# A hybrid attention block: rows of q and k renumbered for their set-down, rotary tables made early

## The chip, the cores and the metric

The kernel runs on one core of a Trainium2 chip. A core has five engines that each work through their own list of instructions in order: TensorE (PE) for matrix products, VectorE (DVE), ScalarE (ACT), GpSimd (POOL) and SyncE (SP), which here issues every transfer (DMA). The engines wait for one another by semaphores. The metric is the device time of one execution in microseconds (us).

## The reference, cut to what matters

The block has two sub-layers over 1024 tokens of width 1024. The first normalises x, scales and shifts it by a vector computed from the conditioning input c (a product with `w_ada`), projects it, and runs two kinds of attention side by side: mixer A (8 query heads, 2 key heads, a sliding window of 128, a sink in the softmax) and mixer B (8 heads, a mixture of three dilated windows). In each head the first 16 of 64 entries of q and k are rotated by the token's position:

```python
def partial_rope(x, cos, sin):
    half = ROT_DIM // 2
    x1 = x[..., :half].astype(jnp.float32)
    x2 = x[..., half:ROT_DIM].astype(jnp.float32)
    rot = jnp.concatenate([x1 * cos - x2 * sin, x2 * cos + x1 * sin], axis=-1).astype(x.dtype)
    return jnp.concatenate([rot, x[..., ROT_DIM:]], axis=-1)
```

The mixers' outputs are normalised, joined and projected, and the result is added to x. The second sub-layer is a squared-ReLU perceptron of width 4096, also scaled, shifted and gated from c. Scores are sums over a head's 64 entries, so the order in which these entries lie in memory is free as long as q and k agree.

## The kernel before, in words

All products are done in split precision: an operand is held as a rounded part (hi) and its rest (lo), and a product is three matmuls, hi x hi, lo x hi and hi x lo (lines 861, 862 and 864 in the projection).

*Front.* The first 36 us or so load x and part of `w_ada`, normalise x (ACT's squares at line 613, POOL's power for the root), transpose it on PE (`pxt`), and form the scale and shift in four groups (`acc_a`, `pm`, `g_a`, `s_a`). ACT and DVE then write the modulated input `hw` (lines 681, 684, 687). While PE has no work, it multiplies ones (`ones_r`).

*Units.* Attention is done in six units: 0 and 1 are mixer A (4 query heads and one key head each), 2 to 5 mixer B (2 heads each). A unit's projection has three column groups c = 0, 1, 2 for each half x of the sequence (512 tokens). The first unit accumulates in six banks at once (`acc`), the others one bank after another (`pj`). Columns are ordered by `_columns()` such that c = 0 holds all entries that are rotated. Weights are loaded (`w_st`), rounded on ACT (line 539) and their rests formed on DVE or POOL (line 544).

*Evacuation and set-down.* `evac` takes each bank to a staging tile (`stage`, five buffers): for c = 0 DVE rotates (lines 757 to 760, with the tables `tabs`), ACT rounds (763), DVE or POOL forms the rest (766); for c = 1 and 2 ACT rounds (774) and DVE forms the rest (777). Then SP moves rows out of the staging tile into `qt` and `kt`, with entries along the partitions and the hi and lo parts in two blocks of 64 partitions (line 803). This is called a set-down below. The staging buffer is free again when its set-down has landed. The lists `PARTS_A` and `PARTS_B` say which staging rows go where: first row, count, step, q or k, first row of the head.

```python
o = dst[64 * i + row:64 * i + row + m_].bitcast(F32)
nc.sync.dma_start(o, src if both else src[:, s_])
```

*Rotary tables.* DVE reduces the angles at the start. `f_sin` takes sine and cosine on ACT and then one exponential, since ACT holds one set of functions at a time and softmax needs the other. POOL writes sine and cosine into row tiles (`rows`, line 713), PE transposes them (`ptab`, line 719) and ACT scales them into `tabs` (721). They are made once for the A units and again for the B units.

*Attention* takes scores (`s_ps`: line 1177 for A, 1122 for B), softmax over DVE, ACT and POOL, transposes (`pt_ps`) and the product with v (`o_ps`); results go to memory by way of `ot` and `o_dram`. POOL also reduces the remaining `w_ada` pieces (`wa_st`, `ada_acc`), whose loads share the staging buffers. After about 560 us the perceptron follows (`mlp_ps`), in which PE is the only limit.

*Order.* No order is written out by hand. The class `Sched` simulates the engines with assumed durations when the program is built, and emits each engine's work in the order of that simulation, so a change in one place shifts the order elsewhere. It counts a transfer by its bytes at one rate, whatever rows it goes to (lines in `load`).

Of the kernel before, what the change touches and what calls it, by code (L numbers as in the profile page):

```python
# [19 lines left out]
P = 128  # L20
# [13 lines left out]
def _split_const(value, top, bits, count):  # L34
    parts, rest, unit = [], value, 2.0 ** (top - bits)
    for _ in range(count):
# [29 lines left out]
PARTS_B = (((0, 64, 2, "q", 0), (1, 64, 2, "k", 0)), ((0, 64, 2, "q", 32), (1, 64, 2, "k", 32)), ())  # L66
PARTS_A = (((0, 32, 2, "q", 0), (64, 32, 2, "q", 32), (1, 64, 2, "k", 0)),
           ((0, 96, 1, "q", 8), (96, 32, 1, "q", 40)), ((0, 64, 1, "q", 48),))

ROWS_B = [*range(0, 8), *range(16, 24), *range(8, 16), *range(24, 64)]  # L70
ROWS_A = [*range(0, 8), *range(16, 40), *range(8, 16), *range(40, 64)]


def _columns():

    out = []
    for u in range(6):
        if u > 1:
            q = [512 + 128 * u + 64 * h for h in range(2)]
            k, v = [x + 512 for x in q], [x + 1024 for x in q]  # L80
            parts, rows = PARTS_B, ROWS_B
        else:
            g = u
            q, k, v = [256 * g + 64 * h for h in range(4)], [512 + 64 * g], [640 + 64 * g]
            parts, rows = PARTS_A, ROWS_A
        for c in range(3):
            got = [h + d for h in v for d in range(64)] if c == 2 else []
            got = [0] * (P - len(got)) + got
            for p, n, step, whose, row in parts[c]:
                heads = q if whose == "q" else k  # L90
                got[p:p + n * step:step] = [h + rows[row + r] for r in range(n // len(heads)) for h in heads]
            out += got
    return out
# [226 lines left out]
def t_sb(n):  # L320
    return 0.098 + 0.00083 * n
# [27 lines left out]
def hybrid_block(ctx: ExitStack, tc: tile.TileContext, x, positions, w_ada, b_ada, g_attn_post, w_in, w_out,  # L349
# [227 lines left out]
    e_cond = op("DVE", 0.52, f_cond, [e], prio=0)  # L577

# [25 lines left out]
    def f_sin():  # L604
        A.activation(sinw[:, :, 1], ang[:], AF.Sin)
        A.activation(cosw[:], kq[:], AF.Sin)
        A.activation(ang[:], kq[:], AF.Exp)
    e_ang, e_xn = e, [[], []]

    def x_block(tb):  # L610
# [4 lines left out]
        e = rsqrt_mean(rstd[:, tb:tb + 1], ssq[:, tb:tb + 1], e)  # L615
        e = op(("ACT", "DVE"), (t_sb(D) + AP_COST, t_d2(D) + AP_DV),
# [77 lines left out]
    for g in range(4):  # L694
        mod_group(g)
    e = op("ACT", 3.2, f_sin, [e_ang] + e_xn[0] + e_xn[1], prio=8)
    e_rope = op("DVE", 0.15, lambda: V.tensor_scalar(sinw[:, :, 0], sinw[:, :, 1], -1.0, None, ALU.mult), [e],
                prio=8)

    def tables(groups, place, r_place, r_bank, bank, deps):  # L700

        for i in range(2):
            b = {}

            def f_rows(i=i, b=b):
                t = b["t"] = place()[:].rearrange("p (b r) -> p b r", b=TB)
                G.memset(t, 0.0 if i else 1.0)
                for o, step, h in groups:
                    for x in range(2):
                        src = sinw[:, :, 1 - x] if i else cosw[:]  # L710
                        o_ = o + 64 * x
                        for j in range(h):
                            G.tensor_copy(t[:, :, o_ + j * step:o_ + j * step + (8 * h - h) * step + 1:h * step], src)
            e = op("POOL", 4.0, f_rows, [e_rope], takes=[(r_place, 1)], prio=0)
            for x in range(2):
# [4 lines left out]
                d = pe_op("tab", 0.43, f_t, [e], takes=[(r_bank, 1)], gives=[(r_place, 1)] if x else [])  # L720
# [5 lines left out]
    tables([(0, 2, 4), (1, 2, 1)], lambda: place0("rows"), r_wa, r_t,  # L726
           lambda: pt.tile([P, 4, P], F32, name="ptab", tag="t"), [[], []])


# [4 lines left out]
    def evac(u, x, c, get_ps, done, r_bank):  # L734
# [47 lines left out]
        if parts:  # L782
            for whose in ("k", "q") if c == 0 else ("q", "k"):
# [5 lines left out]
                for s_ in ((0, 1) if not both else (None,)):  # L789
                    new = c == 0 and whose == "k" and s_ in (0, None)  # L790

                    def f_st(s_=s_, new=new, mine=mine, whose=whose, nh=nh, both=both):
# [5 lines left out]
                        for p0_, n_, step, _, row in mine:  # L798
                            src = b["f"][p0_:p0_ + (n_ - 1) * step + 1:step]
                            m_ = n_ // nh  # L800
                            for i in range(2) if both else (s_,):
                                o = dst[64 * i + row:64 * i + row + m_].bitcast(F32)
# [138 lines left out]
    def feed_proj():  # L941
        if len(sc.pe.get("dense", [])) <= 4 and todo_dense:
# [3 lines left out]
            if (u, x, c) == (2, 0, 0):  # L946
                for e_ in e_tab:
                    e_.clear()
                tables([(0, 1, 4)], lambda: stage("rows"), r_stg, r_x,
# [1125 lines left out]
```

## Time and profile before

| quantity | value |
|---|---|
| median of three runs | 1163.08 us (1161.61 to 1167.61) |
| the profiled execution | 1161.99 us |
| its span in the trace | 1160.2 us |
| PE busy | 1117.1 us, 96% of the span |
| DVE busy | 815.4 us, 70% |
| ACT busy | 639.2 us, 55% |
| POOL busy | 261.1 us, 23% |

The page lists each engine's busy time, the granted clock of PE over the span, the chain of work that ended last, and groups of instructions. Lines such as L803 are lines of the kernel before; in the changed kernel lines behind the first edits are up to five higher. A row in a list of instructions gives start, duration, engine, line, operation and tiles, and in brackets the idle time before it with what ended it. Matmuls overlap, so the duration of one (390 ns) is longer than the distance between two (some 230 ns).

### The profile page before, as it was taken

To read this page: it belongs to the slowest core of one execution; us is meant where nothing else is said; L and a number is where in the kernel's file an instruction comes from. 1 tells how busy PE (TensorE), PEld (TensorE's weight loads), DVE (VectorE), ACT (ScalarE), POOL (GpSimd) and SP (SyncE) were. 2 spreads that over 40 slices of the span, in tenths; PEclk is the share of its full clock that TensorE was granted. 3 is DMA by queue.
4 is the path that set the end of the run, shared out by engine and by line. 5 is a ranking of instruction groups with operands and counts; after the bars stand their busy time and mean duration, and the time that the engine had idled before them with its cause. 6 is when DMAs were issued, how large, how long until landed. Compare 5 with 4: busy or idle time off the path is not lost.

```text
span 1160.2 us, 15646 instructions
## 1 busy us (share of the span) xinstructions
PE 1117.1 (96%) x5416; PEld 926.6 (80%) x5416; DVE 815.4 (70%) x1380; ACT 639.2 (55%) x1105; POOL 261.1 (23%) x344
## 2 busy tenths in 40 slices
PE   8989989999999899998999999999999999999996
PEld 7768778788888787887788888888888888888885
DVE  7848576566666775658969665499653796547998
ACT  7949676455555774667676524563233732246542
POOL 2347667566663441112000000000000000000002
PEclk9989989999999989999999999999999999999998
DMA  9477857465545614554683057812369212585103
GB/s 351 161 174 168 168 120 182 111 153 122 134 102 130 156 48 139 193 181 182 257 314 118 19 207 274 315 50 89 120 220 326 106 55 73 184 306 181 37 19 146
DMA packets 90944, 185.31 MB, mean 160 GB/s; under 512 B 8432, under 2 KB 31088, under 8 KB 90864
## 3 DMA queue, kind: packets, MB, share of 16 engines
q1 hardware_dynamic: 90864, 184.30, 51.1%
q8 instruction: 43, 0.70, 0.3%
q14 instruction: 37, 0.30, 0.1%
HBM read 137.08 MB, written 28.31 MB: 143 GB/s over the span
## 4 chain that ended last, share of the span: by engine, by line
PE 70%; DVE 10%; DMA 7%; issue 4%; POOL 4%; ACT 3%; SPq 2%; DVEq 0%; POOLq 0%; ACTq 0%
PE mlp_ps L1898 16%; PE mlp_ps L1899 16%; PE mlp_ps L1897 16%; PE pj L861 3%; PE pj L864 3%; PE pj L862 3%; PE s_ps L1122 2%; PE o_ps L1257 1%; DMA wa<-in_w_ada 1%; SPq L803 1%; PE pt_ps L1227 1%; DMA wa_st<-in_w_ada 1%; DVE hw L1668 1%; PE pt_ps L1230 1%; PE s_ps L1177 1%
## 5 line engine op out<-in xcount | busy, mean ns | idle before, releaser
L1897 PE MATMUL mlp_ps<-hw 128*128 128x512 f32 x896 | 349.7, 390 | 1.2 <-ACT hw L1659 1.2
L1898 PE MATMUL mlp_ps<-hw 128*128 128x512 f32 x896 | 348.7, 389 | 1.1 <-DVE hw L1665 1.1
L1899 PE MATMUL mlp_ps<-hw 128*128 128x512 f32 x896 | 348.6, 389 | 0.0
L1897 PEld LDWEIGHTS mlp_ps<-hw 128*128 128x128 f32 x896 | 168.2, 188 | 36.8 <-ACT hw L1659 1.6
L1898 PEld LDWEIGHTS mlp_ps<-hw 128*128 128x128 f32 x896 | 168.2, 188 | 36.8 <-DVE hw L1665 1.4
L1899 PEld LDWEIGHTS mlp_ps<-hw 128*128 128x128 f32 x896 | 168.2, 188 | 34.9
L1668 DVE TENSOR_TENSOR hw<-w,hw 128x1024 fp32r<-128x1024 f32 x96 | 114.5, 1219 | 94.7 <-ACT hw L1661 94.4
L1661 ACT CAST hw<-w 128x1024 fp32r<-128x1024 f32 x96 | 97.5, 1047 | 129.8 <-PE mlp_ps L1899 97.5
L1997 POOL TENSOR_TENSOR st<-st,nhalf 128x1 f32<-128x1 f32 x8 | 7.8, 978 | 601.9 <-DVE st L1995 601.9
L861 PE MATMUL pj<-hw,w_hl 128*128 128x512 f32 x240 | 104.2, 434 | 0.0
L864 PE MATMUL pj<-hw,w_hl 128*128 128x512 f32 x240 | 95.5, 398 | 0.0
L862 PE MATMUL pj<-hw,w_hl 128*128 128x512 f32 x240 | 95.3, 397 | 0.0
L1245 DVE TENSOR_TENSOR ph<-pt_ps,ph 128x512 fp32r<-128x512 f32 (+1 forms) x110 | 69.7, 648 | 36.0 <-ACT ph L1241 35.7
L1661 ACT CAST hw<-u 128x1024 fp32r<-128x1024 f32 x48 | 48.7, 1052 | 64.6 <-PE mlp_ps L1899 64.6
L1241 ACT CAST ph<-pt_ps 128x512 fp32r<-128x512 f32 (+1 forms) x110 | 59.5, 555 | 32.1 <-PE pt_ps L1230 27.0
L1668 DVE TENSOR_TENSOR hw<-u,hw 128x1024 fp32r<-128x1024 f32 x48 | 57.0, 1218 | 18.2 <-ACT hw L1661 18.2
L1148 ACT ACTIVATE p_sb<-p_sb,mn 128x128 f32<-128x128 f32 (+3 forms) x64 | 49.7, 777 | 36.3 <-DVE mn L1141 34.9
L1955 DVE TENSOR_TENSOR yacc<-yacc,mlp_ps 128x512 f32<-128x512 f32 x96 | 62.1, 681 | 3.3 <-PE mlp_ps L1899 3.3
L1153 POOL TENSOR_SCALAR p_sb<-p_sb,den 128x128 f32<-128x128 f32 (+3 forms) x64 | 49.0, 775 | 47.8 <-DVE den L1151 44.6
L1010 POOL TENSOR_TENSOR ada_acc<-ada_acc,wa_st 128x512 f32<-128x512 f32 x42 | 55.5, 1320 | 3.5
L864 PEld LDWEIGHTS pj<-hw,w_hl 128*128 128x128 f32 x240 | 45.6, 190 | 10.7
L1473 PE MATMUL y_ps<-hw,oh 128*128 128x512 f32 x128 | 51.7, 404 | 0.0
(205 smaller groups left out, 2010.6 us busy)
## 6 DMA issues: line engine op xcount, KB each, us to landing
hw<-s_dram SPq DMA_DIRECT2D x84, 512.0 KB
wa_st<-in_w_ada SPq DMA_DIRECT2D x32, 512.0 KB
w<-in_w_up SPq DMA_DIRECT2D x32, 512.0 KB
w<-in_w_down SPq DMA_DIRECT2D x32, 512.0 KB
s_dram<-hw SPq DMA_DIRECT2D x28, 512.0 KB
w_st<-in_w_in SPq DMA_DIRECT2D x36, 256.0 KB
x_sb<-in_x SPq DMA_DIRECT2D x16, 512.0 KB
wa<-in_w_ada SPq DMA_DIRECT2D x32, 256.0 KB
```

Of the source, the lines that this page charges most:

```text
L861: T.matmul(ps, w[:, 0, n], h[0], start=(k == 0), stop=False)
L862: T.matmul(ps, w[:, 1, n], h[0], start=False, stop=False)
L864: T.matmul(ps, w[:, 0, n], h[1], start=False, stop=(k == KC - 1))
L1010: G.tensor_tensor(ada.acc[:, :512], ada.acc[:, :512], wa[:, j], ALU.add)
L1241: A.copy(b["ph"][:, 0, :w], b["pt"][:, :w])
L1245: V.tensor_tensor(b["ph"][:, 1, :w], b["pt"][:, :w], b["ph"][:, 0, :w].bitcast(F32), ALU.subtract)
L1661: A.copy(out[j][0], flat(src[j]))
L1668: V.tensor_tensor(out[j][1], flat(src[j]), out[j][0].bitcast(F32), ALU.subtract)
L1897: T.matmul(ps[m][:], sh, mh, start=starts and k == 0, stop=False, **kw)
L1898: T.matmul(ps[m][:], sh, ml_, start=False, stop=False, **kw)
L1899: T.matmul(ps[m][:], sl, mh, start=False, stop=k == 3, **kw)
L1955: e = op("DVE", t_dv(512), lambda: V.tensor_tensor(y(), y(), ps[m][:], ALU.add), [e, ml.e_y[tb, n]], gives=gives, prio=1)
```

## The change

It has two parts.

The rows of q and k are renumbered. hi and lo no longer lie in two blocks of 64 partitions but in turn, row by row, and the rows that one transfer fills are 2, 4 or 8 partitions apart and reach over all 128. A sixth entry in `PARTS_A` and `PARTS_B` gives the distance, `ROWS_A` and `ROWS_B` reorder the weights' columns to match, and the key head of mixer A's rotary rows in the tables moves likewise. For mixer A the two or three pieces of q in a column group become one, so there are fewer transfers; for mixer B their number stays.

The rotary tables are made early. ACT loads the sine functions at the start, ahead of the first square of x, by a small activation on `warm`; `f_sin` follows as soon as the angles are reduced and is without the exponential, which a second small activation fetches behind the last modulation. The tables' row tiles lie in the ring of the values (`vring`) instead of the front's buffers, are written once all roots of x are known, and PE transposes them after the fourth modulated block.

```diff
-PARTS_B = (((0, 64, 2, "q", 0), (1, 64, 2, "k", 0)), ((0, 64, 2, "q", 32), (1, 64, 2, "k", 32)), ())
-PARTS_A = (((0, 32, 2, "q", 0), (64, 32, 2, "q", 32), (1, 64, 2, "k", 0)),
-           ((0, 96, 1, "q", 8), (96, 32, 1, "q", 40)), ((0, 64, 1, "q", 48),))
...
-ROWS_B = [*range(0, 8), *range(16, 24), *range(8, 16), *range(24, 64)]
-ROWS_A = [*range(0, 8), *range(16, 40), *range(8, 16), *range(40, 64)]
+PARTS_B = (((0, 64, 2, "q", 0, 2), (1, 64, 2, "k", 0, 2)), ((0, 64, 2, "q", 1, 2), (1, 64, 2, "k", 1, 2)), ())
+PARTS_A = (((0, 64, 2, "q", 0, 4), (1, 64, 2, "k", 0, 1)), ((0, 128, 1, "q", 1, 2),), ((0, 64, 1, "q", 2, 4),))
+
+FIRST_B = [*range(0, 8), *range(16, 24), *range(8, 16), *range(24, 32)]
+ROWS_B = [FIRST_B[r // 2] if r % 2 == 0 else 32 + r // 2 for r in range(64)]
+ROWS_A = [r // 4 if r % 4 == 0 else 16 + 3 * (r // 4) + r % 4 - 1 for r in range(64)]
...
-            for p, n, step, whose, row in parts[c]:
+            for p, n, step, whose, row, ds in parts[c]:
                 heads = q if whose == "q" else k
-                got[p:p + n * step:step] = [h + rows[row + r] for r in range(n // len(heads)) for h in heads]
+                got[p:p + n * step:step] = [h + rows[row + ds * r] for r in range(n // len(heads)) for h in heads]
...
+    warm = p0.tile([P, KC], F32, name="warm")
+    e_sinset = op("ACT", 1.5, lambda: A.activation(warm[:], nhalf[:], AF.Sin), [e, e_init], prio=0)
...
@@ -604,8 +606,10 @@
     def f_sin():
         A.activation(sinw[:, :, 1], ang[:], AF.Sin)
         A.activation(cosw[:], kq[:], AF.Sin)
-        A.activation(ang[:], kq[:], AF.Exp)
-    e_ang, e_xn = e, [[], []]
+    e_xn, e_rs = [[], []], []
+    e_sin = op("ACT", 0.5, f_sin, [e, e_sinset], prio=1)
+    e_rope = op("DVE", 0.15, lambda: V.tensor_scalar(sinw[:, :, 0], sinw[:, :, 1], -1.0, None, ALU.mult), [e_sin],
+                prio=1)
...
         e = op("ACT", t_sb(D) + AP_COST, f_sq, [x_e[tb]], prio=2)
         e = rsqrt_mean(rstd[:, tb:tb + 1], ssq[:, tb:tb + 1], e)
+        e_rs.append(e)
...
-    e = op("ACT", 3.2, f_sin, [e_ang] + e_xn[0] + e_xn[1], prio=8)
-    e_rope = op("DVE", 0.15, lambda: V.tensor_scalar(sinw[:, :, 0], sinw[:, :, 1], -1.0, None, ALU.mult), [e],
-                prio=8)
...
             def f_rows(i=i, b=b):
-                t = b["t"] = place()[:].rearrange("p (b r) -> p b r", b=TB)
+                t = b["t"] = place(i)
                 G.memset(t, 0.0 if i else 1.0)
...
-            e = op("POOL", 4.0, f_rows, [e_rope], takes=[(r_place, 1)], prio=0)
+            e = op("POOL", 4.0, f_rows, [e_rope] + e_rs, takes=[(r_place, 1)] if r_place else [], prio=0)
             for x in range(2):
                 def f_t(x=x, b=b):
                     b[x] = bank()
                     for j in range(4):
                         T.transpose(b[x][:, j], b["t"][:, 4 * x + j], ident)
-                d = pe_op("tab", 0.43, f_t, [e], takes=[(r_bank, 1)], gives=[(r_place, 1)] if x else [])
+                d = pe_op("tab", 0.43, f_t, [e, e_hh[3, 1]], takes=[(r_bank, 1)], gives=[(r_place, 1)] if x and r_place else [])
...
-    tables([(0, 2, 4), (1, 2, 1)], lambda: place0("rows"), r_wa, r_t,
+    tables([(0, 2, 4), (1, 8, 1)], lambda i: vring.tile([P, TB, P], F32, name="rows", tag="v"), r_v, r_t,
            lambda: pt.tile([P, 4, P], F32, name="ptab", tag="t"), [[], []])
...
+    op("ACT", 1.6, lambda: A.activation(warm[:], nhalf[:], AF.Exp), [e_sin] + [e_hl[KC - 1, x] for x in range(2)],
+       prio=8)
...
                         dst = qs[u, x][:] if whose == "q" else ks[u][:, :, cs]
-                        for p0_, n_, step, _, row in mine:
+                        for p0_, n_, step, _, row, ds in mine:
                             src = b["f"][p0_:p0_ + (n_ - 1) * step + 1:step]
                             m_ = n_ // nh
                             for i in range(2) if both else (s_,):
-                                o = dst[64 * i + row:64 * i + row + m_].bitcast(F32)
+                                o = dst[2 * row + i:2 * row + i + 2 * ds * (m_ - 1) + 1:2 * ds].bitcast(F32)
                                 nc.sync.dma_start(o, src if both else src[:, s_])
...
-                tables([(0, 1, 4)], lambda: stage("rows"), r_stg, r_x,
+                tables([(0, 1, 4)], lambda i: stage("rows")[:].rearrange("p (b r) -> p b r", b=TB), r_stg, r_x,
                        lambda: px.tile([P, 4, P], F32, name="ptab", tag="x"), [[e_rot[1, 0]], [e_rot[1, 1]]])
```

How the order of instructions moves shows at three places. The first is SP's queue, the set-down of the first unit (kt and qt are k and q as scores read them, hl the staging tile; sizes are partitions x elements). Before, for the first half, from the masks on:

```order
L971 DMA masks<-in_consts 128x1280
L530 DMA w_st<-in_w_in 128x512
L994 DMA wa_st<-in_w_ada 128x2x512
L803 DMA kt<-hl 64x2x512 x2
L803 DMA qt<-hl 8x4x512 x4
L803 DMA qt<-hl 24x4x512
L803 DMA qt<-hl 8x4x512
L803 DMA qt<-hl 24x4x512
L803 DMA qt<-hl 8x4x512
L803 DMA qt<-hl 16x4x512 x2
```

Now, for the same half:

```order
L976 DMA masks<-in_consts 128x1280
L530 DMA w_st<-in_w_in 128x512 x3
L808 DMA kt<-hl 64x2x512 x2
L808 DMA qt<-hl 16x4x512 x2
L808 DMA qt<-hl 32x4x512 x2
L808 DMA qt<-hl 16x4x512 x2
```

Twelve issues become eight, the load of the next `w_ada` piece goes behind both halves' set-downs, and the masks go ahead of two more weight loads.

The second is PE at the first scores. Before (pj is the next unit's projection, pv the transpose of values):

```order
L861 MATMUL pj<-hw,w_hl 128x512
L862 MATMUL pj<-hw,w_hl 128x512
L864 MATMUL pj<-hw,w_hl 128x512
L1177 MATMUL s_ps<-kt,qt 128x128 x8
L861 MATMUL pj<-hw,w_hl 128x512
L862 MATMUL pj<-hw,w_hl 128x512
```

Now:

```order
L866 MATMUL pj<-hw,w_hl 128x512
L867 MATMUL pj<-hw,w_hl 128x512
L869 MATMUL pj<-hw,w_hl 128x512
L836 MATMUL pv<-head,vt 128x64 x4
L1182 MATMUL s_ps<-kt,qt 128x128 x8
L866 MATMUL pj<-hw,w_hl 128x512
```

Between the first unit's last product and these scores stand 42 matmuls of pj before and 21 now; the other 21 follow behind. The four groups of `ptab` transposes, before among the last 36 products of the first unit, now all stand ahead of the last 98.

The third is ACT, where the sine and cosine were taken (cond is the conditioning vector, junk the output of the squares that is not used). Before, between two modulations:

```order
L539 CAST w_hl<-w_st 128x512 x2
L605 ACT_TABLE_LOAD
L605 ACTIVATE sinw<-ang 128x8x8
L606 ACTIVATE cosw<-kq 128x64
L607 ACT_TABLE_LOAD
L607 ACTIVATE ang<-kq 128x64
```

Now, at the start of the program:

```order
L571 ACTIVATE cond<-head 128x8
L579 ACT_TABLE_LOAD
L579 ACTIVATE warm<-nhalf 128x8
L617 ACTIVATE junk,ssq<-x_sb 128x1024 x2
L622 ACTIVATE x_sb<-x_sb,rstd 128x1024
L607 ACTIVATE sinw<-ang 128x8x8
L608 ACTIVATE cosw<-kq 128x64
```

The two loads of function sets are no longer between modulations: one is at the front, and the other stands behind the last modulation (line 732). On POOL four weight rests (line 544) stand ahead of the first rest of q and k, where there were two.

## The prediction

> **What bounds the kernel now.** I read the page first: busy time by engine and the shares of the chain of work that ended last.
>
> ```profile
> PE 1117.1 (96%) x5416; PEld 926.6 (80%) x5416; DVE 815.4 (70%) x1380; ACT 639.2 (55%) x1105; POOL 261.1 (23%) x344
> PE 70%; DVE 10%; DMA 7%; issue 4%; POOL 4%; ACT 3%; SPq 2%; DVEq 0%; POOLq 0%; ACTq 0%
> ```
>
> TensorE (PE) is the bound on the average, so the change can only earn what PE loses now. Next I read PE's waits between 60 and 230 us (in total, times, longest), the stretch in which q's and k's parts of the first units are set down:
>
> ```profile
> PE s_ps L1177 <- DMA kt<-hl: 5.5, 1, 5.5
> PE pv L831 <- ACT tab L721: 5.0, 1, 5.0
> PE pv L831 <- DVE ot L1293: 2.5, 1, 2.5
> PE o_ps L1269 <- DVE ph L1245: 0.6, 1, 0.6
> PE pt_ps L1234 <- POOL p_sb L1209: 0.3, 1, 0.3
> ```
>
> Three stalls stand out. The table by stretches shows what lies around them (columns: stretch, its length, busy time of PE, PEld, DVE, ACT, POOL, then granted clock, DMA share, GB/s):
>
> ```profile
> 36.00:77.00 41.00, 41.00 (x197) 33.88 (x198) 27.44 (x43) 27.96 (x37) 20.57 (x33) 1.00 0.52 152
> 80.93:87.76 6.83, 4.76 (x16) 3.75 (x17) 4.62 (x14) 2.75 (x10) 1.76 (x3) 0.50 0.70 158
> 88.00:143.00 55.00, 54.49 (x316) 46.00 (x315) 40.15 (x126) 44.19 (x128) 40.68 (x77) 1.00 0.80 170
> 145.79:152.61 6.82, 3.90 (x16) 3.50 (x17) 4.41 (x14) 4.55 (x13) 6.60 (x11) 0.50 0.39 99
> 207.23:210.64 3.41, 2.94 (x11) 2.65 (x12) 2.26 (x4) 1.80 (x4) 3.33 (x4) 0.50 0.34 79
> ```
>
> Before, between and behind the stalls PE is busy nearly without a gap (41.00 of 41.00, 54.49 of 55.00). Each stall is followed by a stretch at half the granted clock, so its price is the wait plus half of PE's busy time there: 5.5 + 2.4 = 7.9, 5.0 + 1.95 = 7.0 and 2.5 + 1.5 = 4.0 us, 18.9 in all.
>
> [...] The third wait is 2.5 us and the clock fell. [...]
>
> What ended the three waits is in the chain (start, us, what):
>
> ```profile
> 78.45 4.46 DMA kt<-hl
> 83.00 1.94 PE s_ps L1177 x8
> 135.32 8.68 DMA qt<-hl
> 144.02 0.33 ACT hl L774
> 148.71 0.69 PE pv L831 x4
> 201.62 5.50 DMA o_dram<-ot
> 207.23 0.43 DVE ot L1293
> 207.70 1.12 PE pv L831 x4
> ```
>
> All three end with a slow transfer: a set-down of k, a set-down of q that holds a staging buffer ScalarE (ACT) needs, and a store queued behind set-downs. Why they are slow shows in two neighbouring stretches of PE-bound time, the first while q's transfers into 32 adjacent rows drain, the second while weights arrive in all 128 rows:
>
> ```profile
> 232.90:236.90 4.00, 4.00 (x23) 3.44 (x23) 1.77 (x7) 1.29 (x3) 0.00 (x0) 1.00 1.02 125
> 237.90:240.30 2.40, 2.40 (x15) 2.00 (x14) 1.19 (x3) 2.01 (x5) 1.06 (x2) 1.00 1.05 400
> ```
>
> The DMA engines are fully busy in both (1.02, 1.05), yet move 125 GB/s in one and 400 in the other.
>
> **The change, part by part.** *Rows renumbered.* The first unit is set down by these issues on SyncE's queue (SP):
>
> ```profile
> 67.47 1.78 SPq L803 DMA_DIRECT2D kt<-hl  x2
> 69.31 8.35 SPq L803 DMA_DIRECT2D qt<-hl  x10
> 77.75 1.32 SPq L803 DMA_DIRECT2D kt<-hl  x2
> 79.16 7.46 SPq L803 DMA_DIRECT2D qt<-hl  x10
> ```
>
> The new order has 2 + 6 issues for each half instead of 2 + 10, at some 0.65 us each (1.32 for two): 5.2 us instead of 8 to 10. That is four halves in the two units of mixer A, 16 issues fewer. Mixer B's units keep theirs. The bytes stay: 2 of 256 KB for k, 4 of 128 and 2 of 256 for q, 1.57 MB for a half. New rate: the rows written are now 2, 4 or 8 apart over all partitions. Its bounds are the two rows above, 125 (nothing gained) and 400 GB/s (as good as a load into all rows). I take 250, about their middle, since a set-down also reads on-chip memory. A half then moves in 6.3 us instead of 12.6 at 125 and 3.9 at 400.
>
> [...]
>
> *Tables early.* Rotation (VectorE, DVE) waited for the sine table, and what it released went on over ACT and GpSimd (POOL) to the first set-down:
>
> ```profile
> 57.58 1.29 DVE L544 TENSOR_TENSOR w_hl<-w_st,w_hl 128x512 fp32r<-128x512 f32 x2
> 62.57 0.68 DVE L757 TENSOR_TENSOR hl<-acc,tab 64x512 f32<-64x512 f32 x1 [3.70 <-ACT tab L721]
> 65.45 0.62 ACT L763 CAST hl<-hl 128x512 fp32r<-128x512 f32 x1 [1.07 <-DVE hl L760]
> 66.15 1.30 POOL L766 TENSOR_TENSOR hl<-hl 128x512 fp32r<-128x512 f32 x1 [1.74 <-ACT hl L763]
> ```
>
> Of the 3.70 us I count 2.4. The four groups of table transposes (some 0.6 us each on PE) move ahead of the last products, so the same PE time comes earlier, and the first product ends about 1 us later than its 59.5. The first set-down is then issued at 67.5 - 2.4 = 65.1.
>
> ACT and POOL, which it moves the work past:
>
> ```profile
> 4.35 0.21 ACT L571 ACTIVATE cond<-head 128x8 f32<-128x8 f32 x1 [2.35 <-DMA head<-in_consts]
> 5.60 1.06 ACT L613 ACTIVATE junk<-x_sb 128x1024 bf16<-128x1024 f32 x1 [1.05 <-DMA x_sb<-in_x]
> 41.13 1.28 ACT L605 ACT_TABLE_LOAD   x1
> 42.84 1.28 ACT L607 ACT_TABLE_LOAD   x1
> 42.96 4.77 POOL L713 COPY rows<-cosw 128x64 f32<-128x64 f32 x10 [9.00 <-ACT cosw L606]
> 61.67 1.29 POOL L544 TENSOR_TENSOR w_hl<-w_st,w_hl 128x512 fp32r<-128x512 f32 x1 [8.04 <-ACT w_hl L539]
> 0.00:40.00 40.00, 35.88 (x181) 28.41 (x182) 32.04 (x76) 33.59 (x52) 8.92 (x21) 1.00 0.95 335
> ```
>
> The sine load goes ahead of the first square of x, where 1.05 us were free; it and the two sines push x's chain back by up to 1.3 us. DMA was 0.95 busy in the first 40 us, so loads hide most of this; I charge 0.5 (0 to 1.3). The exponential's load goes behind the last modulation, where ACT waits for weights: 0. POOL copies the rows from about 29 us in its idle time: 0. POOL also takes two more weight splits ahead of the first rest of q and k (1.29 each); they fall into its 8.04 us of idle time: 0. If the weights came late there, they would hold the set-down, as a rival below has it.
>
> *First stall.* From 65.1, eight issues end at 70.3; an undisturbed 256 KB landing takes 2.7 us after its issue begins:
>
> ```profile
> 58.90 2.69 DMA w_st<-in_w_in
> ```
>
> So the half has landed at about 72.4. PE ends the first unit's products at 67.2 as before and has 21 projection matmuls (0.23 each) and the value transposes ahead of the scores, so it arrives at 72.5. I leave 1.0 of the 7.9: gain 6.9 (0 to 7.9).
>
> *Second stall.* The last transfer took 8.68 us; halving what lies over 2.69 gives 5.7, 3.0 us less. Idle 5.0 becomes 2.0, and I count half of the clock's 1.95: gain 4.0 (0 to 7.0).
>
> *Third stall.* Halving again, 5.50 becomes 4.1, so 1.4 us, and with a wait of 1.1 the clock stays: gain 2.9 (0 to 4.0).
>
> *What is late next.* With PE early, softmax's chain through DVE, ACT and POOL has less slack. PE's other waits in that stretch sum to 0.9 us; I charge 2.0 (0 to 8, POOL being busy 40.68 of 55 us).
>
> Sum: -6.9 - 4.0 - 2.9 + 2.0 + 0.5 = -11.3 us. The profiled execution took 1162.0 (span 1160.2 and 1.8 around it), which gives 1150.7, say 1151; it stands 1.1 below the median of the runs, 1163.1.
>
> **Rivals.**
> - *Everything goes.* All three stalls end and nothing new comes: 1162 - 18.9 = 1143. For it: PE's full stretches. Against: ACT and POOL work in order and wait for landings whatever the rate.
> - *Transfers don't speed up.* Something other than adjacent rows limits them. Half a unit then lands near 77; the score matmuls start 6 us earlier but with 21 instead of 42 projection matmuls done (4.8 us). Only 16 issues and little else are left: 1160. For it: k and q both come from on-chip memory, unlike the 400 GB/s load.
> - *POOL becomes the bound.* It is 74% busy from 88 to 143, and the weight reduction it also does waits for loads now queued behind the set-downs. The 8 us end of that term: 1157.
> - *Slower.* Rows 4 and 8 apart make the writes worse, or the late weights hold the first set-down. PE has only 21 matmuls of cover, so from a landing after 78.2 (83.0 - 4.8) on it loses; that is below 1.57 MB in 11 us, 140 GB/s. Landing at 83 as now costs the 4.8, and a longer stay at half clock 1: 1168. Against it: nothing in the trace is slower than the adjacent rows.
>
> **How the numbers follow.** Forecast 1146 to 1157, 0.45; everything goes 0.20; no faster transfers 0.15; POOL 0.10; slower 0.10. The range 1141 to 1161 leaves out the slower case and the best end of the second, with their tails 2 in 10. A measurement tells 0.5%, 5.8 us, from no change, so faster means below 1157.3: nearly all of the forecast, the second case, half of POOL's, together 0.70. Same 0.19: most of the third and the rest of POOL's. Slower 0.11.
>
> **What would show it.** Right: no PE wait over 2 us at the first score matmuls, the full clock from 60 to 230 us, over 200 GB/s while set-downs drain, and rotation begun near 60 us. Wrong: DMA full at 125 GB/s while q is set down, half clock near 80 us, first score matmuls after 78 us, or POOL ending PE's waits.
>
> The issues, the 21 and the 42 are read from the orders of SP and PE shown with the change above.

## The result, and the profile after

The changed kernel takes 1148.5 us (median of four runs, 1147.7 to 1149.0), the kernel before, run beside it, 1162.3. The ratio is 0.9865, with a 95% interval of 0.9838 to 0.9892: faster by 1.1 to 1.6%. The forecast was 1151, and faster. The profiled execution took 1148.9 us, 13.1 less than that of before (1162.0), with a span of 1147.1.

Busy time by engine and the shares of the chain of work that ended last, of the kernel after:

```profile
PE 1115.2 (97%) x5417; PEld 924.1 (81%) x5417; DVE 818.7 (71%) x1380; ACT 635.9 (55%) x1101; POOL 265.7 (23%) x349
PE 76%; DVE 8%; issue 4%; ACT 4%; POOL 4%; DMA 3%; SPq 1%; DVEq 0%; POOLq 0%; ACTq 0%
```

The work is the same. Transfers fell from 7 to 3% of the chain, VectorE from 10 to 8%, and TensorE (PE) rose from 70 to 76%. PE's waits between 60 and 230 us (in total, times, longest) are now:

```profile
PE s_ps L1182 <- DVE mn L1197: 1.8, 1, 1.8
PE pv L836 <- DVE ot L1298: 0.7, 1, 0.7
...
PE s_ps L1182 <- DMA qt<-hl: 0.2, 1, 0.2
```

The stalls of 5.5 and 5.0 us are gone, and of the third, 2.5 us, 0.7 is left. Four stretches read so after: the set-down of the first half, the long PE-bound stretch, and two that ran at half the clock before (stretch, length, busy time of PE, PEld, DVE, ACT, POOL, granted clock, DMA share, GB/s):

```profile
66.45:74.10 7.65, 7.46 (x37) 5.51 (x35) 4.65 (x8) 4.12 (x8) 4.35 (x7) 1.00 0.75 268
88.00:143.00 55.00, 54.29 (x308) 45.09 (x307) 39.70 (x116) 44.93 (x126) 44.88 (x82) 1.00 0.56 166
145.79:152.61 6.82, 5.04 (x29) 4.08 (x28) 6.68 (x17) 4.01 (x11) 5.51 (x8) 1.00 0.11 35
207.23:210.64 3.41, 3.41 (x23) 2.98 (x22) 3.41 (x7) 0.99 (x2) 2.43 (x3) 1.00 0.12 43
```

While the first half is set down, 268 GB/s move, and the engines are not full (0.75). From 88 to 143 us nearly the same traffic (166 GB/s, 170 before) keeps the DMA engines busy for 0.56 of the time where it was 0.80: the transfers move as much in less time.

Where the 13.1 us come from shows stage by stage. Both kernels, before first, then after:

```profile
60.00:100.00 40.00, 34.48 (x176) 28.55 (x176) 22.65 (x67) 21.76 (x61) 21.79 (x33) 0.91 0.80 190
100.00:180.00 80.00, 73.82 (x405) 60.96 (x404) 54.12 (x155) 60.00 (x165) 53.57 (x93) 0.96 0.69 155
180.00:230.00 50.00, 47.48 (x254) 39.52 (x253) 32.41 (x82) 26.74 (x57) 34.45 (x37) 0.97 0.54 126
480.00:560.00 80.00, 74.54 (x350) 60.50 (x348) 60.16 (x96) 54.04 (x85) 12.25 (x13) 1.00 0.49 178
```

```profile
60.00:100.00 40.00, 39.62 (x220) 33.56 (x219) 29.54 (x87) 28.51 (x82) 27.40 (x42) 1.00 0.61 196
100.00:180.00 80.00, 77.28 (x421) 63.17 (x420) 57.55 (x161) 57.95 (x156) 60.02 (x98) 1.00 0.53 161
180.00:230.00 50.00, 48.85 (x273) 41.14 (x272) 29.41 (x73) 25.41 (x53) 32.49 (x36) 1.00 0.43 147
480.00:560.00 80.00, 74.74 (x333) 60.72 (x332) 64.19 (x92) 52.85 (x79) 10.45 (x10) 0.96 0.49 181
```

PE's idle time is the length less its busy time: 5.5, 6.2, 2.5 and 5.5 us before, 0.4, 2.7, 1.2 and 5.3 after. The half clock is gone from the first three stages, and a new one stands in the fourth (0.96).

For all kernels of this study I worked out PE's loss by stage from the matmuls' records: idle time (from the end of one to the start of the next) plus half of what PE was busy at half clock. The names are those of the experiments below; the last column is the profiled execution's time less the loss.

```
us              0-60  60-100 100-180 180-230 230-300 300-480 480-560  560-   sum   time   rest
before           4.1     7.9     8.2     4.0     0.6    10.9     6.1   0.0  41.8  1162.0  1120.2
after            4.9     0.4     2.7     1.2     0.3    10.4     8.3   0.0  28.2  1148.9  1120.7
e1_rows_only     4.0     6.0     8.7     0.4     0.2    11.7     7.1   0.0  38.1  1157.6  1119.5
e2_tables_only   5.5     9.8     6.4     7.5     0.8     8.2     4.1   4.0  46.3  1169.2  1122.9
e3_blocks        5.4     9.2     2.7     2.3     0.8    10.2     6.2   0.0  36.9  1157.3  1120.4
e4_before_turns  3.8     2.5     2.6     4.6     0.8    10.7     6.2   0.0  31.0  1152.9  1121.9
e6_A_only        5.6     0.5     2.4     7.1     4.2     8.7     7.1   0.0  35.6  1157.0  1121.4
e7_B_only        4.2    12.2     8.0     1.4     0.7     9.9     5.6   1.5  43.7  1164.6  1120.9
e8_tables_turns  5.2     1.8     3.0     4.6     1.7    10.1     7.1   0.0  33.5  1155.6  1122.1
e10_twelve       5.5     4.6     2.9     0.5     0.3    10.7     8.3   0.0  32.8  1155.0  1122.2
```

The rest is 1119.5 to 1122.9 in all ten, so PE's losses account for the differences to within some 2 us, and a kernel's loss can be read stage by stage. Between before and after the first set-downs bring 7.5, the next stage 5.5 and the third 2.8 us; the front costs 0.8 and the stage from 480 to 560 us 2.2.

### The profile page after: what moved, and what is told of

Same layout as the page of the kernel before. It is cut to its first block, busy times and chain, and to the rows that moved or that the text cites. A ratio compares the mean times of both kernels' runs of the same rounds, so it can differ in the third digit from the quotient of the medians.

```text
span 1147.1 us, 15609 instructions
## 1 busy us (share of the span) xinstructions
PE 1115.2 (97%) x5417; PEld 924.1 (81%) x5417; DVE 818.7 (71%) x1380; ACT 635.9 (55%) x1101; POOL 265.7 (23%) x349
## 4 chain that ended last, share of the span: by engine, by line
PE 76%; DVE 8%; issue 4%; ACT 4%; POOL 4%; DMA 3%; SPq 1%; DVEq 0%; POOLq 0%; ACTq 0%
PE mlp_ps L1903 16%; PE mlp_ps L1904 16%; PE mlp_ps L1902 16%; PE pj L866 3%; PE pj L869 3%; PE pj L867 3%; PE s_ps L1127 3%; PE o_ps L1262 2%; PE pt_ps L1232 1%; PE y_ps L1478 1%; PE y_ps L1480 1%; PE y_ps L1479 1%; PE pt_ps L1235 1%; DVE hw L1673 1%; PE o_ps L1267 1%
## 5 line engine op out<-in xcount | busy, mean ns | idle before, releaser
L866 PE MATMUL pj<-hw,w_hl 128*128 128x512 f32 x240 | 102.5, 427 | 0.0
L869 PE MATMUL pj<-hw,w_hl 128*128 128x512 f32 x240 | 94.6, 394 | 0.0
L867 PE MATMUL pj<-hw,w_hl 128*128 128x512 f32 x240 | 94.5, 394 | 0.0
```

What stands on the lines that cost most here:

```text
L866: T.matmul(ps, w[:, 0, n], h[0], start=(k == 0), stop=False)
L867: T.matmul(ps, w[:, 1, n], h[0], start=False, stop=False)
L869: T.matmul(ps, w[:, 0, n], h[1], start=False, stop=(k == KC - 1))
```

## The experiments

Medians are used where kernels are compared. The kernel before had medians of 1162 to 1166 us in the different sets of runs, so kernels of different sets are compared by their ratio to it, and 1% is then 11.6 us. The expectations name theories by number or content; the two questions throughout are which part of the change carries the gain, and by what property of the transfers.

**One part alone.** The first kernel is the one before with the rows renumbered and the tables late:

```diff
-PARTS_A = (((0, 32, 2, "q", 0), (64, 32, 2, "q", 32), (1, 64, 2, "k", 0)),
-           ((0, 96, 1, "q", 8), (96, 32, 1, "q", 40)), ((0, 64, 1, "q", 48),))
+PARTS_A = (((0, 64, 2, "q", 0, 4), (1, 64, 2, "k", 0, 1)), ((0, 128, 1, "q", 1, 2),), ((0, 64, 1, "q", 2, 4),))
...
-                                o = dst[64 * i + row:64 * i + row + m_].bitcast(F32)
+                                o = dst[2 * row + i:2 * row + i + 2 * ds * (m_ - 1) + 1:2 * ds].bitcast(F32)
```

> The kernel before with the renumbered rows and without the early tables: sine and cosine are taken between modulations as before. Theory 1 (the rows: transfers into spread rows are faster and fewer): most of the gain is here, 1148 to 1153 us, with no half clock between 60 and 230 us. Theory 2 (the early tables, and the new order they bring): little is left, 1157 to 1162 us, and PE still waits over 3 us at the first scores.

Measured: 1157.0 us, ratio 0.9923 (0.9897 to 0.9948). Neither theory fits: the median stands at the lower edge of theory 2's range, but the first scores wait 2.1 us, not over 3; and half clock follows them, which theory 1 ruled out. The second is the kernel with the tables early and the old rows:

```diff
+    e_sin = op("ACT", 0.5, f_sin, [e, e_sinset], prio=1)
...
-    tables([(0, 2, 4), (1, 2, 1)], lambda: place0("rows"), r_wa, r_t,
+    tables([(0, 2, 4), (1, 2, 1)], lambda i: vring.tile([P, TB, P], F32, name="rows", tag="v"), r_v, r_t,
```

> The kernel before with the early tables and the old rows. Theory 1 (the rows): 1158 to 1165 us, with the wait at the first scores still there; the 30 projection matmuls that now stand ahead of them instead of 42 could make that wait longer. Theory 2 (the tables): 1149 to 1155 us.

Measured: 1172.1 us, ratio 1.0052 (1.0026 to 1.0079): slower, which neither theory had. The parts don't add: 0.77% gained and 0.52% lost alone, 1.35% gained together.

Why the rows alone fall short shows in PE's waits between 60 and 230 us in the first of the two:

```profile
PE s_ps L1177 <- DMA o_dram<-ot: 4.9, 1, 4.9
PE s_ps L1177 <- DMA qt<-hl: 2.6, 2, 2.1
```

and in SyncE's (SP's) queue ahead of that store:

```profile
131.42 6.72 SPq L803 DMA_DIRECT2D qt<-hl  x2
144.18 0.39 SPq L994 DMA_DIRECT2D wa_st<-in_w_ada  x1
144.65 0.56 SPq L803 DMA_DIRECT2D qt<-hl  x1
145.30 2.58 SPq L1314 DMA_DIRECT2D o_dram<-ot  x4
```

SP issued nothing from 138.1 to 144.18, when a `w_ada` load got the buffer that POOL's reduction held. The set-down and the stores behind it waited with it, and PE's scores for the stores. In the changed kernel a `w_ada` load waits for its buffer there too (2.9 us, issued at 139.46), but no store that PE needs stands behind it.

The first scores (the 2.6 us above hold their wait of 2.1) are late in this kernel for another reason. From 62.84 us on the masks, two weight loads and a `w_ada` load go out just ahead of the first set-down, which starts at 67.06. In the changed kernel the masks are ahead at 54.47, and the `w_ada` load goes out at 78.09, behind both halves. The last of these loads, then the time to landing of the first half's set-downs:

```profile
64.46 0.44 SPq L994 DMA_DIRECT2D wa_st<-in_w_ada  x1
DMA to landing us min/median/max: 4.6/5.1/5.3
```

The same set-downs in the changed kernel take 2.6 (shown below). So the two stages in which this kernel falls behind, 60 to 100 and 100 to 180 us, both show loads in the way, in the order that the planner made. In the first, half clock adds 3.4 us to the wait. That is read from the traces; no run moved one of these loads alone.

**The reach of the rows.** The next kernel is the changed one, with the same instructions in the same order, and only hi and lo back in two blocks of 64 partitions (with the distances of 1, 2 and 4 within a block):

```diff
-                                o = dst[2 * row + i:2 * row + i + 2 * ds * (m_ - 1) + 1:2 * ds].bitcast(F32)
+                                o = dst[64 * i + row:64 * i + row + ds * (m_ - 1) + 1:ds].bitcast(F32)
```

> The changed kernel, same instructions in the same order, but hi and lo again in two blocks of 64 partitions: the rows of one transfer are 1, 2 or 4 apart inside one half of the partitions instead of 2, 4 or 8 apart over all. Theory 1a (the reach over all partitions sets the rate): set-downs move at about half the rate, the first half lands some 3 us later, and the time is 1151 to 1157 us. Theory 1b (fewer and larger transfers do it, wherever the rows lie): 1148 to 1150 us.

Measured: 1159.3 us, ratio 0.9944 (0.9929 to 0.9959), 0.79% or 9.2 us over the changed kernel's ratio and 2 us beyond theory 1a's range; 1b is refuted. The set-downs of the first half (issues, their durations in ns, then time to landing), first with the blocks, then in the changed kernel:

```profile
L808 SPq DMA_DIRECT2D qt<-hl x6: 554/574/713, 68.7 to 72.0; - x6
DMA to landing us min/median/max: 4.3/6.2/7.6
```

```profile
L808 SPq DMA_DIRECT2D qt<-hl x6: 550/569/602, 68.2 to 71.5; - x6
DMA to landing us min/median/max: 2.5/2.6/2.8
```

Issues go out at the same pace; landings take 6.2 us in place of 2.6. PE then waits again, at the value transposes and the scores:

```profile
PE pv L836 <- ACT vt L830: 3.2, 1, 3.2
PE s_ps L1182 <- DMA qt<-hl: 2.1, 1, 2.1
```

The mirror of it is the kernel before, unchanged in instructions and order, with nothing but hi and lo in turn, so that 8 to 64 rows reach over 16 to 128 partitions:

```diff
-                                o = dst[64 * i + row:64 * i + row + m_].bitcast(F32)
+                                o = dst[2 * row + i:2 * row + i + 2 * m_ - 1:2].bitcast(F32)
```

> The kernel before, same instructions in the same order, but hi and lo rows in turn: each transfer's rows are 2 apart instead of adjacent, so 8 rows span 16 partitions. k reaches all partitions, q's 32 rows span 64. Theory 1a (reach sets the rate): part of the gain, 1153 to 1160 us, with the wait at the first scores under 4 us. Theory 1b (count and size of transfers): 1160 to 1164 us, and the waits stay.

Measured: 1152.5 us, ratio 0.9892 (0.9878 to 0.9907), a little better than theory 1a had it. One line of addresses gives 1.08% of the 1.35%; what the rest of the change adds, 0.27%, is not clear of noise, as the two intervals overlap. The first stall falls from 7.9 to 2.5 and the second stage from 8.2 to 2.6 in the table of losses; the stage from 180 to 230 us stays.

**The rates by themselves.** A kernel without the block's work moves bundles of set-downs in on-chip memory, one kind after the other:

```diff
+    ("adj32", slice(0, 32), 2048, (slice(0, 128, 2), 1024), 8),
+    ("by4_32", slice(0, 128, 4), 2048, (slice(0, 128, 2), 1024), 8),
...
+                    nc.sync.dma_start(d[j][rows, 0:n], src[i][ps, 0:w])
```

> A kernel that computes nothing of the block: after one load of x and sixteen clears, it does eight bundles of set-downs within on-chip memory, one bundle after the other, VectorE reading the results in between, and nothing else beside them. The bundles differ in the destination rows: 32 adjacent (8 transfers of 256 KB), 32 rows 4 apart (the same bytes), 8 adjacent (16 of 64 KB), 16 adjacent, 16 rows 4 apart, 16 rows 8 apart (16 of 128 KB each), 64 adjacent and 64 rows 2 apart (8 of 256 KB). Source rows are 2 apart in all. Theory (the destination's reach sets the rate): 32 adjacent at about 125 GB/s as in the trace of before, 32 rows 4 apart at 200 to 400, so a bundle of 2.1 MB in 17 us against 5 to 10; the same pair ratio, 1.6 to 3, for 64 rows and for 16 rows. [...] Rival (the source or the size of pieces limits, the destination doesn't): all bundles within 20% of each other.

The steady part of each bundle, in the order of the expectation (stretch, length, busy time of DVE and POOL, clock, DMA share, GB/s):

```profile
12.50:20.70 8.20, 6.70 (x5) 0.00 (x0) 1.00 0.96 128
45.80:51.00 5.20, 4.07 (x4) 0.00 (x0) 1.00 0.98 393
69.30:75.36 6.06, 5.89 (x6) 0.00 (x0) 1.00 0.56 55
84.50:98.90 14.40, 13.96 (x12) 0.00 (x0) 1.00 1.10 109
107.00:113.40 6.40, 6.23 (x6) 0.00 (x0) 1.00 0.71 205
128.50:135.20 6.70, 6.53 (x6) 0.00 (x0) 1.00 0.73 196
153.20:163.10 9.90, 6.13 (x5) 0.00 (x0) 1.00 1.04 132
167.50:171.40 3.90, 2.65 (x3) 0.00 (x0) 1.00 1.00 399
```

Adjacent rows give 55, 109, 128 and 132 GB/s for 8, 16, 32 and 64 of them; spread rows 393 and 399 with 256 KB a transfer, 205 and 196 with 128 KB. The spread ones come at the pace of SP's issues: the eight transfers into 32 rows 4 apart take 5.07 us, 0.63 each, and 256 KB in 0.63 us are 416 GB/s, 128 KB 208. In the first bundle each transfer also waited for its tile to be cleared, one in 2.14 us; the DMA engines were 0.96 busy all the same, so its 128 is low by a few per cent at most.

```profile
44.49 5.07 SPq L84 DMA_DIRECT2D d<-src  x8
```

So a spread set-down of 128 KB costs its issue: the engines are only 0.71 to 0.73 busy. With 256 KB they are full as well (0.98 and 1.00), and these rows can't say which of the two limits.

**One mixer alone.** The changed kernel with mixer B's rows as before, then with mixer A's as before (there with four more issues in each half, not five more pieces as the expectation counts):

```diff
-                                o = dst[2 * row + i:2 * row + i + 2 * ds * (m_ - 1) + 1:2 * ds].bitcast(F32)
+                                o = dst[64 * i + row:64 * i + row + m_] if isb else dst[
+                                    2 * row + i:2 * row + i + 2 * ds * (m_ - 1) + 1:2 * ds]
+                                o = o.bitcast(F32)
```

> The changed kernel with mixer B's rows as before (two blocks, 32 adjacent rows a transfer) and mixer A's rows spread; same instructions in the same order. Theory (each mixer's stalls hang on its own transfers): stalls 1 and 2 stay gone, stall 3 near 205 us comes back with up to 4.0 us, and later set-downs of mixer B wait more: 1151 to 1155. Rival (only the first unit counts, since later set-downs have slack): 1148 to 1150, no wait over 1 us near 205. Third possibility (B's spread carries most of the 10 us that both blocks cost together): 1156 or more.

> Tables early and mixer B's rows spread, mixer A's rows as before (8 to 64 adjacent rows in two blocks, five pieces more in a half); same instructions in the same order as with the tables alone (1172.1). Theory: the stalls of the first unit and the second half of A stay as with the tables alone, and only the waits near 205 us and later go: 1165 to 1170, half clock near 80 us. Rival (B's spread carries the gain): 1160 or less.

Measured: 1155.6 us with A spread alone (ratio 0.9910, 0.9885 to 0.9936) and 1165.0 with B alone (0.9991, 0.9975 to 1.0007). Against the tables alone (1.0052) A brings 1.42% and B 0.61%; put in last, A brings 1.26% and B 0.45%. So with the tables early the two add up: A some 16, B some 6 us. A's share holds its fewer issues too. For A alone the median lies 0.6 us above the theory's range, half a microsecond short of the third possibility; for B alone it lies at the lower end of the theory's range. B is worth more than the third stall: without its spread the stage from 180 to 230 us loses 7.1 us in place of 1.2, and the next one, to 300 us, 4.2 in place of 0.3 (table of losses).

**The tables with a wide reach.** Tables early, hi and lo in turn, rows otherwise numbered as before (the difference to the kernel with the tables alone):

```diff
-                                o = dst[64 * i + row:64 * i + row + m_].bitcast(F32)
+                                o = dst[2 * row + i:2 * row + i + 2 * m_ - 1:2].bitcast(F32)
```

> Tables early and hi and lo in turn, rows otherwise numbered as before, so the pieces of q stay many (12 issues a half) and reach 16 to 128 partitions; same instructions in the same order as with the tables alone (1172.1). Theory (the early tables lose alone because the slow set-downs then collide with weights, and are harmless or of use with a wide reach): 1148 to 1153, as good as the whole change within its interval, and below the 1152.5 that the same address change gave without the tables. Rival (the early tables cost 6 us whatever the transfers do, and the whole change is better because it has fewer issues): 1157 to 1162. Third (the order is what it hangs on, by luck): anything else, and then the waits have to say which.

Measured: 1158.0 us, ratio 0.9934 (0.9912 to 0.9956). My theory falls and the rival holds in the time, though its reason, the number of issues, does not carry it, as the next experiment shows: here too the early tables cost, 0.42% against the same kernel with late tables, much as with the old rows (0.52%). Only with the renumbered rows do they gain, 0.58% (from 0.9923 to 0.9865), and there the kernel with late tables has the loads in the way that were shown above.

**The number of issues.** The changed kernel with k's transfers and q's of the second column group cut in two, so that a half of mixer A has 12 issues again, to the same rows. (Before, its column groups had two, two and one piece of q, not two or three each; hi and lo make ten issues of them, and k two.)

```diff
+                            cut = 2 if not isb and n_ // nh >= 32 else 1
+                            n_, m_ = n_ // cut, n_ // nh // cut
+                            for j in range(cut):
+                                p1, r1 = p0_ + j * n_ * step, row + j * m_ * ds
...
```

> The changed kernel, with k's transfers and q's of the second column group in mixer A's units cut in two: 12 issues for a half as before instead of 8, the same bytes to the same rows, everything else in the same order. Theory (a spread transfer takes no longer than its issue, 0.65 us, so a half is as long as its issues are many): the first half lands 4 x 0.65 = 2.6 us later, near 76.7, TensorE waits 2.6 us more at the first scores with some half clock behind: 1151 to 1155. That would be part of why the tables with many pieces in turns took 1158. Rival (landing times hang on the bytes, and the issues lie beside them): 1148 to 1150.

Measured: 1155.7 us (1151.4 to 1156.6), ratio 0.9919 (0.9887 to 0.9950), 0.54% over the changed kernel. The queue of SP, then PE's two waits at the first scores:

```profile
67.55 2.99 SPq L811 DMA_DIRECT2D kt<-hl  x4
70.59 5.07 SPq L811 DMA_DIRECT2D qt<-hl  x8
```

```profile
PE s_ps L1185 <- DMA qt<-hl: 1.6, 1, 1.6
PE pv L839 <- ACT vt L833: 1.5, 2, 1.3
```

The first half's issues end at 75.66 in place of 72.08. Of these 3.6 us 1.1 were there before the first issue (67.55 after 66.45), and the four issues make the other 2.5. PE loses 4.6 us from 60 to 100 where it lost 0.4; 1.7 of it is half clock. So fewer issues do help here, and the rival is out, though the median lies 0.7 us above the theory's range and the interval still overlaps the changed kernel's.

This does not account for what the early tables with many pieces lacked (0.9934, also 12 issues a half). By the table of losses that kernel loses 1.8 us from 60 to 100 and 4.6 from 180 to 230, this one 4.6 and 0.5. The stage from 180 to 230 us goes with mixer B's rows: its loss is 0.4 to 1.4 us in the four kernels in which they reach over all partitions (after, e1, e7, e10), 2.3 to 4.6 where a transfer reaches over half of them (e3, e4, e8), and 4.0 to 7.5 where its rows lie side by side (before, e2, e6).

**The clock.** Half-clock stretches come and go between these kernels where their waits are alike: one of 3.02 us before kept the full clock, the same one of 3.06 us after did not (both are shown in the last section). So PE runs bursts of matmuls with waits of eight lengths between them, in a kernel without the block's work:

```diff
+                for i in range(n):
+                    nc.vector.tensor_copy(b[1 - i % 2][:], b[i % 2][:])
+                nc.vector.tensor_copy(a[:, :256], b[n % 2][:])
+                for _ in range(m):
+                    nc.tensor.matmul(ps[:], w[:], a[:], start=True, stop=True)
```

> A kernel that computes nothing of the block: TensorE runs bursts of 30 to 45 matmuls of 128x512, and between them waits for a chain of VectorE copies of eight lengths, seven times each, about 0.9 to 4 us, at shifting places in time. Theory (the clock is decided window by window, 3.41 us each on a grid that nothing in the program sets: with about 2 us idle in one window the next one runs at half): waits under 1.5 us never drop the clock, waits over 3.6 us nearly always do, and those of 2 to 3.6 us do or don't by where they fall; told apart by idle time per window, at least 9 in 10 windows with over 2.0 us are followed by half clock and at most 1 in 10 of those under 1.5 us. [...]

How many of seven waits of each length were followed by half clock, and, with the time cut into the 3.41 us steps on which the clock changed, how many of those steps at full clock were followed by one at half (both worked out from the records of matmuls and clock):

```
wait, us          0.84  1.50  1.83  2.16  2.49  2.81  3.47  4.12
then half clock    0/7   0/7   3/7   4/7   3/7   6/7   7/7   7/7

idle in a step    under 1.75   1.75 to 2.0   2.0 and more
then half clock        0/134          6/11          24/24
```

Waits of one length behave differently, idle time per step tells them apart: the theory holds for these bursts. In the ten kernels of the block all 20 steps at full clock with 2.0 us idle or more were followed by half clock too, but so were 13 with 1.28 to 1.99. In the one with 1.28 (mixer A spread alone, at 285.47 us) 1.05 us of the busy time are eight matmuls of a single column; whether such short matmuls count as busy for the clock was not tested.

## Why the prediction was right

**The bound and the prices of the stalls: right.** Forecast were 7.9, 7.0 and 4.0 us as the stalls' whole price. The table of losses has 7.9, 8.2 and 4.0 in these three stages, and all ten kernels' times follow such losses to within 2 us. That the rows' reach sets the transfers' time, the ground of the forecast, is shown by the two kernels that change nothing but addresses: the first half's set-downs land in 6.2 us with the blocks where they took 2.6, and hi and lo in turn bring the kernel before to 0.9892 of its time.

**The new rate: too low, without harm.** I took 250 GB/s between 125 and 400. The measured rate alone is 393 to 399, so the true value stood at the upper bound; the reason I set against it, that a set-down also reads on-chip memory, does not show in that rate, whose transfers do so too. It did no harm because the half's landing was reckoned by the issues all the same: eight in 5.2 us and one landing behind them. That gave 7.3 us from the first issue to the last landing (65.1 to 72.4). The trace has the first issue at 66.45 and the first scores, which a q transfer of this half released, at 74.30, 7.9 us later:

```profile
73.65 0.46 PE pv L836 x4
74.11 0.19 issue
74.30 1.08 PE s_ps L1182 x8
```

**The first set-down's time: 1.4 us too early.** Forecast 65.1, measured 66.45, in these steps:

```profile
61.31 0.68 DVE L762 TENSOR_TENSOR hl<-acc,tab 64x512 f32<-64x512 f32 x1 [1.96 <-PE acc L869]
63.87 1.29 POOL L544 TENSOR_TENSOR w_hl<-w_st,w_hl 128x512 fp32r<-128x512 f32 x1 [2.13 <-ACT w_hl L539]
64.19 0.63 ACT L768 CAST hl<-hl 128x512 fp32r<-128x512 f32 x1 [0.40 <-DVE hl L765]
65.12 1.30 POOL L771 TENSOR_TENSOR hl<-hl 128x512 fp32r<-128x512 f32 x1
66.45 1.38 SPq L808 DMA_DIRECT2D kt<-hl  x2
```

Rotation waits for the product and not for the table any more, as forecast, but it begins 1.1 us later than the 60.2 that the 2.4 us gave: the product ends at 61.3, 1.8 us after its 59.5, where I had about 1. That 1 alone already left no more than 2.1 of the 2.4. A weight's rest, which I costed at nothing, holds POOL 0.3 us past the end of ACT's rounding. Rotation gained 1.3 us here, not 2.4, and the first issue 1.0.

**First stall: forecast 6.9, measured 7.5.** PE too arrived later than 72.5, at 74.1, when the landing came. Both errors are of one size and cancel, which is luck.

**Second stall less what is late next: forecast 2.0 (4.0 less 2.0), measured 5.5.** This is the sum's largest error. The transfers did not stay half slow, as "halving what lies over 2.69" had it; the wait of 5.0 and its half clock are gone altogether. What comes late next is softmax (1.8 us at L1197), as said; the charge of 2.0 is about that wait, and no other came near it. POOL was busier from 88 to 143 us (44.88 of 55.00 us; 40.68 before) and did not become the bound.

**Third stall: forecast 2.9, measured 2.8.** The size is right. Its transfer was to go from 5.50 to 4.1; the store at the same place in the chain now takes 3.28.

```profile
190.01 3.28 DMA o_dram<-ot
```

The forecast's wait of 1.1 is the 1.2 lost in this stage, of which the wait on `ot` is 0.7; the clock stayed, at 1.00.

**The front: forecast 0.5, measured 0.8.** In the table the kernels with early tables lose 4.2 to 5.6 us before 60, those with late ones 3.8 to 4.1.

**The rate's rival, "transfers don't speed up": refuted** by the two kernels that change nothing but addresses. **"Everything goes", 1143: nearly so in the three stages** (4.3 of the losses of 20.1 remain); these 4.3, a step of the clock near 530 us and the front keep the time from it.

**The sum: close in part by luck.** The three stalls less what is late next brought 15.8 us where 11.8 were forecast. Against that stand the front, 0.3 more than forecast, and 2.2 us from 480 to 560 that no term had; what is left over is 0.3. So -11.3 and the measured -13.1 lie closer together than their terms do.

**What I had not seen.** I priced the tables as a gain of their own, by 2.4 us at the first set-down, with 0.5 against it. In the profiles the first set-down is issued at 67.1 to 67.6 in the three kernels with late tables and at 66.1 to 67.6 in the seven with early ones, 0.5 us sooner on average, and before 60 us the early ones lose 1.2 more. Alone the tables lose 0.52%, and 0.42% beside transfers that are fast but many. The forecast came out because the parts were made together. In all seven kernels with early tables the planner puts the `w_ada` load behind both halves, in the three others ahead of the first; beside the small head start, that is what the traces show in the tables' favour. Which of the planner's choices make up the rest, per stage as the table has it (7.5 us at 180 to 230 with the tables alone, 4.0 before), stays open.

## What to carry to other kernels

Transfers of 256 KB into 32 adjacent partitions ran at 128 GB/s, a third of the 393 of the same transfers spread over all of them; where the order of rows is free, spread it, and then count issues, since each took 0.63 us of SP's queue in the bundles. Add up TensorE's idle time and half of its half-clock time by stage: if time less that sum is the same in all versions, every difference can be placed. A part of a change that lowers one wait may lose alone in a planned kernel, so judge parts in the company in which they ship.

## What the runs showed of the hardware that was not expected

The clock changed on steps of 3.41 us, and a wait's length alone did not decide it. In the kernel before it was at half from 80.93, 145.79 and 207.23 us on, for 6.83, 6.82 and 3.41 us, and the times at full clock between, 58.03 and 54.62 us, are 17 and 16 steps. One wait for the second sub-layer's normalised rows was 3.02 us before and 3.06 us after:

```profile
546.62 1.09 PE L1536 MATMUL px<-head,xn 128*128 128x128 f32 x8 [3.02 <-ACT xn L1527]
```

```profile
531.63 1.97 PE L1541 MATMUL px<-head,xn 128*128 128x128 f32 x8 [3.06 <-ACT xn L1532]
```

Before, the clock stayed; after, it fell for 6.83 us. Before, the wait lay half in one step and half in the next; after, most of it lay in one. The steps, before and then after:

```profile
541.70:545.10 3.40, 1.90 (x9) 1.24 (x7) 3.29 (x5) 0.48 (x1) 3.17 (x1) 1.00 0.38 155
545.10:548.50 3.40, 1.88 (x13) 1.71 (x14) 1.19 (x4) 3.08 (x5) 0.28 (x1) 1.00 0.00 0
```

```profile
527.50:530.91 3.41, 1.07 (x5) 0.56 (x3) 2.50 (x3) 0.48 (x1) 2.90 (x1) 1.00 0.15 59
530.91:537.73 6.82, 6.10 (x19) 5.13 (x20) 3.69 (x10) 5.30 (x7) 0.00 (x0) 0.50 0.00 0
```

Idle time of 1.50 and 1.52 us in a step left the clock, 2.3 us dropped it, as in the bursts (24 of 24 from 2.0 us on, some six tenths of a step; the block's kernels also have drops after less, as said there). So a stall of 2.5 to 3.1 us cost nothing more (the wait of 3.02), or half of what PE was busy at half clock behind it, by where it fell: 1.5 us behind the third stall of before (one step), 3.05 behind the wait of 3.06 (two steps); what part of the spread between runs of one kernel (1160.8 to 1170.1 for the one before) comes from that was not measured.

Bundles into 32 and 64 adjacent rows moved at nearly one rate, 128 and 132 GB/s, though 16 reached 109 and 8 reached 55. What limited them is open.
